# A fourth buffer for the halves of the projections' weights, and a ring of raw tiles that uses its first two tiles twice at its begin

## The chip, the cores and the metric

The kernel runs on one core of a Trainium2 chip. Its time is what the device takes for one execution, in microseconds (us). The median of three executions counts, and a change is looked at as the difference of two medians.

## The reference

A decoder layer over 1024 positions with a width of 1024. Three branches (an mLSTM, a differential attention, a cross-attention into 256 memory tokens) are each projected, weighted by a gate of their own and added, then an output projection and a residual follow, then an MLP with four times the width.

```python
g_m, g_d, g_c = jnp.split(jax.nn.sigmoid(h @ w_gate[l] + b_gate[l]), N_BRANCH, axis=-1)
merged = g_m * (y_m @ w_proj_m[l]) + g_d * (y_d @ w_proj_d[l]) + g_c * (y_c @ w_proj_c[l])
x = x + merged @ w_out[l]
h2 = rms_norm(x, norm_mlp_g[l])
x = x + jnp.square(jax.nn.relu(h2 @ w_up[l])) @ w_down[l]
```

The change touches what stands here: the three projections, the output projection, and the two products of the MLP. All of it is float32.

## The kernel before, in words

**Products in three.** Every float32 operand is split into a high part, a cast to fp32r on ScalarE, and a low part, the subtraction of that cast on VectorE (`split`, lines 111 and 112, and `split2`, lines 104 and 67, which keeps to the order of the program). A product is three matmuls: high with high, high with low, low with high (`mm3`, all at line 91). A weight or an operand is usable when both engines have passed it.

**The projections** (`tail`, from line 1410). There are sixteen groups: four for each of three branches, then four of the output projection. The weights of a group, 1024 x 256, come in two halves of four k each (`load_w`, line 130): SyncE loads a raw half (`raw`, two buffers, pool `rp2`), then it is split into a tile `w` (three buffers of 8 KB per partition, pool `wp2`, line 1445). I count the halves from 0 to 31, so a group uses halves 2g and 2g + 1, and half n takes the buffer n modulo 3. A group computes four tiles of 128 x 512, and each runs over all eight k: the first half of the weights is read until the middle of the fourth tile, the second to its end. Only the first group of each branch runs over k on the outside, since its eight tiles of y come in one by one (`k_tiles`, line 1376, `kraw` with two buffers, `kt`). In front of the sums of a branch a tile of gates is loaded (`gl`, two buffers), in the output projection one of x. There the residual sum is formed (`res`, line 1470, VectorE at line 1474), stored as x1, squared and added to `ssq` on GpSimd, and stored once more, weighted by the norm's gain, as h2. Sums have all eight banks of PSUM to go round.

**The up projection** (`wino`, line 1287) multiplies blocks of 2 x 2 with seven products in the place of eight. A step takes a raw weight tile of four blocks (`wraw`, SyncE, line 1272), forms four sums of them on GpSimd (`wino_s`, lines 1258 to 1261), splits seven (`wo`), and then runs 21 matmuls. I call the split weights W[0] to W[63] after their steps. An operand X[k], k from 0 to 3, is made of h2's rows of two tiles: a load (`xr`, one buffer), four differences (`wino_t`, lines 1240 to 1243), and two splits (`xo`). Run 0 has two steps (X[0], X[1]), run 1 four (X[0] to X[3]), run 2 two (X[2], X[3]), all further runs four. A run fills seven banks, and the eighth moves on by one from run to run. In run 0 the row sums of `ssq` go into the eighth bank (`px`), `st` (line 1531) copies them out, and the next run's first product uses that bank. After a run, VectorE combines its banks (`combine`, the tiles `u` and `c`), scales, and ScalarE applies the square of relu; the result is transformed like X and stored as an operand of the down projection (`r_d`).

**The down projection** (`down`, line 1558) does the same over 64 steps with three buffers for raw and split weights; its operands `xd` are read back from `r_d`. The first operand has three parts in three pools (`dx00`, `dx01`, `dx02`).

**Memory.** Pools lie one behind the other, and a pool of a later stage takes the place of those before. The raw tiles of w_up go round in four places, wr0 to wr3. wr0 and wr1 lie where the raw tiles of y (`kraw`) were, wr2 and wr3 lie in the last of the operands that the output projection reads to its end. The split weights lie in wop1 and three tiles of wop2; those three begin where the raw halves were and reach over the first two buffers of `wp2`. `xo0` and `xo1` (X[0] and X[1]) lie where the tiles of y were, `xo2` and `xo3` in operands of the output projection. In the down projection `dx02` takes the place of wr2 and wr3, and the first two raw tiles of w_down that of wr0 and wr1.

**Order.** A scheduler puts the instructions of the unpinned parts (the projections, and the begin of both products of the MLP) into an order for each engine, by when it thinks operands and buffers free; each engine then works its queue in that order. Within `wino` and `down` TensorE, VectorE and the casts are pinned to the order of the program.

Of the kernel before, what the change touches and what calls it, by code (L numbers as in the profile page):

```python
# [35 lines left out]
class Banks:  # L36


    def __init__(self, enter, name):
        self.pools = [enter(name=f"{name}{i}", bufs=1, space=PSUM) for i in range(8)]  # L40

    def tile(self, shape, dt, tag, name):
        return self.pools[int(tag[-1])].tile(shape, dt, tag=tag, name=name)


class Ring:


    def __init__(self, pools):
        self.pools, self.i = pools, -1  # L50

    def tile(self, *a, **k):
        self.i += 1
        return self.pools[self.i % len(self.pools)].tile(*a, **k)

# [16 lines left out]
class Layer:  # L72
# [487 lines left out]
    def m_gates2(self, pool):  # L560
# [5 lines left out]
        self.nc.vector.tensor_copy(self.gcol, ps2[:, 0 : 3 * W])  # L566

    def branch_m(self, pool, gp, tail, gnext):
        nc, a = self.nc, self.a
        V, G = nc.vector, nc.gpsimd  # L570
# [839 lines left out]
    def tail(self):  # L1410
# [11 lines left out]
        with ExitStack() as c0:  # L1422
            E = lambda *x, **k: c0.enter_context(tc.tile_pool(*x, **k))
# [8 lines left out]
            with ExitStack() as c1:  # L1432
                E = lambda *x, **k: c1.enter_context(tc.tile_pool(*x, **k))
                self.pmm, self.kmm, self.nmm = Banks(E, "pmm2"), 8, 3
                if True:
# [6 lines left out]
                    ysp = Ring([E(name=f"ys{i}", bufs=1) for i in range(9)][::-1])  # L1442
                    rawp = E(name="yrp", bufs=2)
                    self.rp = E(name="rp2", bufs=2)
                    self.wp = E(name="wp2", bufs=3)
                    hi = [[mtp.tile([P, 512], F32R, name=f"mh{k}_{hf}") for hf in range(2)] for k in range(NK)]
                    mg, lo = {}, {}
                    for bi, b in enumerate((2, 0, 1)):
# [41 lines left out]
            with ExitStack() as c1:  # L1490
                E = lambda *x, **k: c1.enter_context(tc.tile_pool(*x, **k))
# [4 lines left out]
                )  # L1496
                wop2 = [one_(f"wop2{i}") for i in range(3)]
                self.xop = (xo0, xo1, xo2, xo3)
                self.wrp, self.wop = Ring([wr0, wr1, wr2, wr3]), Ring([wop1, *wop2])
                dp, ap = one_("dgp"), one_("prt")  # L1500

                def load(kp):
# [395 lines left out]
```

## Time and profile before

| what | us |
|---|---|
| median of three executions | 2201.62 |
| lowest and highest of them | 2198.82, 2202.04 |
| the profiled execution | 2204.73 |
| its span, first to last instruction | 2203.0 |
| mean granted clock of TensorE in it | 0.995 of full |

The profile is that of one execution. PE is TensorE, PEld its weight loads, DVE VectorE, ACT ScalarE, POOL GpSimd, SP SyncE, and the q behind a name is an engine's own queue (issues of transfers). A row of the timeline has the start and the time from there to the end of the last instruction, the engine, the line, the operation, the tiles out<-in, the count, and in brackets the idle time before it with what ended it. Starts are us from the span's begin. The projections run from 1205.98, the output projection from about 1474, the up projection from 1565.70, the down projection from 1884.53.

### The profile page before, as it was taken

Reading aid. Unit: us, or ns where it says so; the run is one execution under the profiler, and the core shown is the slowest. Engines: PE = TensorE matmul, PEld = TensorE weight load, DVE = VectorE, ACT = ScalarE, POOL = GpSimd, SP = SyncE. Lnnn points to the kernel's source line nnn. Section 1 sums busy time; section 2 is a strip of 40 time slices with the busy share of each in tenths; the row PEclk is TensorE's granted clock in tenths of the full one; section 3 lists DMA queues with packets and bytes.
Section 4 is the critical chain, followed back from the end, with each engine's and each line's share of the span. In section 5 each row is a group of like instructions: output and inputs, shape, how many; then the busy total and the mean of one; then the engine's idle time right before and its main releaser. Section 6 shows DMA issues by size and latency. Waiting matters only on the chain.

```text
span 2203.0 us, 30700 instructions
## 1 busy us (share of the span) xinstructions
PE 2154.4 (98%) x11049; PEld 1853.4 (84%) x11049; DVE 1422.5 (65%) x2678; ACT 1002.2 (45%) x1998; POOL 561.1 (25%) x732
## 2 busy tenths in 40 slices
PE   7999999999999999999999999999999999999999
PEld 5878888898899999999887788887787888788887
DVE  6643565575547877877655332544689877767789
ACT  6543354454346666666554220323444444543332
POOL 2100000000111111111121002202657655565553
PEclk9999999999999999999999999999999999999999
DMA  7123122121443343333343543436435444854444
GB/s 250 31 78 110 59 92 68 47 79 48 169 107 92 96 96 97 87 78 88 115 149 130 181 154 114 143 106 210 149 111 199 158 147 147 323 196 153 144 142 169
DMA packets 137358, 281.46 MB, mean 128 GB/s; under 512 B 13137, under 2 KB 29814, under 8 KB 135158
## 3 DMA queue, kind: packets, MB, share of 16 engines
q1 hardware_dynamic: 130870, 259.58, 37.5%
q10 hardware_dynamic: 6336, 19.93, 2.2%
q8 instruction: 87, 1.43, 0.3%
q14 instruction: 65, 0.53, 0.1%
HBM read 182.95 MB, written 71.34 MB: 115 GB/s over the span
## 4 chain that ended last, share of the span: by engine, by line
PE 81%; DMA 6%; DVE 6%; ACT 3%; issue 2%; POOL 1%; SPq 0%; DVEq 0%; ACTq 0%; POOLq 0%
PE mm L91 47%; PE p L91 22%; PE sc L91 6%; PE po L91 3%; PE tp L94 3%; DMA kraw<-y 1%; DVE acc L67 1%; DVE w L112 1%; PE pr L94 1%; DVE wo L67 1%; DVE u L67 0%; PE tp L91 0%; DMA gl<-in_xT 0%; DMA x_d<-gl 0%; DVE xts L67 0%
## 5 line engine op out<-in xcount | busy, mean ns | idle before, releaser
L91 PE MATMUL mm<-w,hT 128*128 128x384 f32 (+3 forms) x2496 | 473.2, 332 | 3.5 <-ACT w L111 3.0
L91 PE MATMUL mm<-hT,w 128*128 128x512 f32 x1680 | 411.9, 396 | 0.0
L91 PEld LDWEIGHTS mm<-w,hT 128*128 128x128 f32 x2496 | 390.2, 190 | 15.4 <-ACT w L111 3.9
L91 PEld LDWEIGHTS mm<-hT,w 128*128 128x128 f32 x1680 | 308.5, 188 | 64.7
L91 PE MATMUL p<-xo,wo 128*128 128x512 f32 x1344 | 309.8, 392 | 6.4 <-DVE st L1531 3.5
L91 PE MATMUL p<-xd,wo 128*128 128x512 f32 x1344 | 309.0, 392 | 4.8 <-DVE u L67 2.0
L91 PEld LDWEIGHTS p<-xo,wo 128*128 128x128 f32 x1344 | 252.2, 189 | 62.6 <-ACT pt L1344 3.9
L91 PEld LDWEIGHTS p<-xd,wo 128*128 128x128 f32 x1344 | 253.4, 189 | 60.2 <-DVE u L67 2.8
L91 PE MATMUL mm<-kt,w 128*128 128x512 f32 x1152 | 264.5, 391 | 5.1 <-ACT kt L111 3.5
L91 PEld LDWEIGHTS mm<-kt,w 128*128 128x128 f32 x1152 | 216.8, 189 | 52.7 <-ACT kt L111 4.3
L111 ACT CAST w<-raw 128x256 fp32r<-128x256 f32 (+3 forms) x272 | 142.1, 545 | 163.3 <-PE mm L91 122.5
L112 DVE TENSOR_TENSOR w<-raw,w 128x256 fp32r<-128x256 f32 (+3 forms) x272 | 161.8, 616 | 75.6 <-ACT w L111 74.9
L104 ACT CAST wo<-wraw 128x896 fp32r<-128x896 f32 x122 | 115.0, 944 | 209.5 <-PE p L91 110.2
L67 DVE TENSOR_TENSOR wo<-wraw,wo 128x896 fp32r<-128x896 f32 x122 | 143.6, 1194 | 59.3 <-ACT wo L104 59.3
L1258 POOL TENSOR_TENSOR wraw<-wraw 128x128 f32<-128x128 f32 x128 | 94.2, 736 | 246.6 <-DMA wraw<-in_wdown 119.8
L1006 ACT ACTIVATE dpe<-sc,dst,drr 128x256 f32<-128x256 f32 (+7 forms) x128 | 106.6, 833 | 97.6 <-DVE dst L1002 95.3
L127 POOL TENSOR_SCALAR hss<-hss 128x4 f32<-128x4 f32 x8 | 3.3, 407 | 416.8 <-ACT mscr L752 273.1
L998 DVE CUSTOM_DVE_ANT_0 sc<-sc,tmask 128x256 f32<-128x256 f32 (+7 forms) x128 | 97.0, 758 | 13.1 <-PE sc L91 12.4
L91 PE MATMUL sc<-dk,dq 128*128 128x512 f32 (+3 forms) x384 | 92.2, 348 | 0.0
L1261 POOL TENSOR_TENSOR wraw<-wraw 128x128 f32<-128x128 f32 x128 | 87.0, 680 | 10.0
L1260 POOL TENSOR_TENSOR wraw<-wraw 128x128 f32<-128x128 f32 x128 | 88.6, 692 | 0.0
L104 ACT CAST xd<-xd 128x1536 fp32r<-128x1536 f32 (+2 forms) x36 | 54.9, 1528 | 69.9 <-DMA xd<-r_d 69.9
(308 smaller groups left out, 3086.0 us busy)
## 6 DMA issues: line engine op xcount, KB each, us to landing
dk<-dsg SPq DMA_DIRECT2D x64, 256.0 KB, 4.5
wraw<-in_wup SPq DMA_DIRECT2D x64, 256.0 KB, 3.2
r_d<-xts SPq DMA_DIRECT2D x16, 1024.0 KB, 4.1
wraw<-in_wdown SPq DMA_DIRECT2D x64, 256.0 KB, 3.0
xd<-r_d SPq DMA_DIRECT2D x19, 768.0 KB, 7.2
xd<-r_d SPq DMA_DIRECT2D x14, 1024.0 KB, 6.7
raw<-in_wd SPq DMA_DIRECT2D x32, 384.0 KB, 3.2
kraw<-y SPq DMA_DIRECT2D x24, 512.0 KB, 4.2
```

The source lines that it names most:

```text
L67: return self.tc.keep_in_program_order(f(*a, **k))
L91: self.pin(self.nc.tensor.matmul(out, l, r, start=start, stop=stop))
L94: self.pin(self.nc.tensor.transpose(out, x, self.ident))
L104: self.A.copy(hi, src)
L111: nc.scalar.copy(hi, src)
L112: nc.vector.tensor_sub(lo, src, f32(hi))
L127: g.tensor_scalar(r, ss, 1.0 / width, EPS, op0=ALU.mult, op1=ALU.add)
L998: V.tensor_tensor_reduce(out=sc[:, 0:n], in0=sc[:, 0:n], in1=self.tmask[:, D - n : D], scale=1.0, scalar=-3.0e38, op0=ALU.add, op1=ALU.max ...
L1006: nc.scalar.activation(pe[c][:, 0:n], sc[:, 0:n], AF.Exp, bias=t8[:, 2 + c : 3 + c], scale=rr[:, i, c : c + 1], accum_out=t8[:, 4 + c : 5 ...
L1258: G.tensor_add(r[:, 4], r[:, 0], r[:, 3])
L1260: G.tensor_sub(r[:, 6], r[:, 1], r[:, 0])
L1261: G.tensor_sub(r[:, 7], r[:, 2], r[:, 5])
```

## The change

The pool `wp2` gets four buffers, so half n takes the buffer n modulo 4. And the ring of the raw tiles of w_up starts again after its first two tiles, once: wr0, wr1, wr0, wr1, wr2, wr3, wr0 and so on, where it went wr0, wr1, wr2, wr3, wr0. The other rings keep their order. All of `wp2`'s fourth buffer lies behind the last pool of the stage, so no other pool moves.

```diff
     def __init__(self, pools, again=0):
-        self.pools, self.i = pools, -1
+        self.pools, self.i, self.again = pools, -1, again

     def tile(self, *a, **k):
+        if self.i == self.again - 1:
+            self.i, self.again = -1, 0
         self.i += 1
         return self.pools[self.i % len(self.pools)].tile(*a, **k)
...
-                    self.wp = E(name="wp2", bufs=3)
+                    self.wp = E(name="wp2", bufs=4)
...
-                self.wrp, self.wop = Ring([wr0, wr1, wr2, wr3]), Ring([wop1, *wop2])
+                self.wrp, self.wop = Ring([wr0, wr1, wr2, wr3], 2), Ring([wop1, *wop2])
```

The change itself is in buffers alone; what it moves is seen in the order. Line numbers are higher by two in the changed kernel. First VectorE between the first and the second group of the output projection, before; w_15103 and w_15108 are the third group's halves, gl_ are residual sums, xts and xo belong to X[0].

```order
L112 TENSOR_TENSOR w_14958<-raw_14956,w_14958 128x1024
L1474 SCALAR_TENSOR_TENSOR gl_14915<-mm_14815,gl_14915 128x512
L1474 SCALAR_TENSOR_TENSOR gl_14923<-mm_14816,gl_14923 128x512
L112 TENSOR_TENSOR w_15103<-raw_15101,w_15103 128x1024
L1474 SCALAR_TENSOR_TENSOR gl_14931<-mm_14817,gl_14931 128x512
```

And further on in the same queue, before, behind X[0]:

```order
L112 TENSOR_TENSOR xo_15522<-xts_15517,xo_15522 128x4x512
L1474 SCALAR_TENSOR_TENSOR gl_15091<-mm_15066,gl_15091 128x512
L112 TENSOR_TENSOR w_15108<-raw_15106,w_15108 128x1024
L112 TENSOR_TENSOR w_15253<-raw_15251,w_15253 128x1024
L1474 SCALAR_TENSOR_TENSOR gl_15136<-mm_15111,gl_15136 128x512
```

The same two places after the change:

```order
L114 TENSOR_TENSOR w_15103<-raw_15101,w_15103 128x1024
L1476 SCALAR_TENSOR_TENSOR gl_14915<-mm_14815,gl_14915 128x512
L1476 SCALAR_TENSOR_TENSOR gl_14923<-mm_14816,gl_14923 128x512
L114 TENSOR_TENSOR w_15108<-raw_15106,w_15108 128x1024
L1476 SCALAR_TENSOR_TENSOR gl_14931<-mm_14817,gl_14931 128x512
```

```order
L114 TENSOR_TENSOR xo_15522<-xts_15517,xo_15522 128x4x512
L1476 SCALAR_TENSOR_TENSOR gl_15091<-mm_15066,gl_15091 128x512
L114 TENSOR_TENSOR w_15253<-raw_15251,w_15253 128x1024
L114 TENSOR_TENSOR w_15258<-raw_15256,w_15258 128x1024
L114 TENSOR_TENSOR wo_15527<-wraw_15509,wo_15527 128x7x128
```

Each half has moved up by about one place of its kind: w_15108 stands where w_15103 stood, and the last half (w_15258) and the split of W[1] (wo_15527), which followed further on, stand behind X[0].

Next SyncE at the end of the output projection, before; wraw_15530 and wraw_15560 are the raw tiles of W[2] and W[3], xr_15675 the load for X[3].

```order
L1484 DMA h_d<-h_2487_15363 128x512
L1272 DMA wraw_15530<-in_wup 128x512
L1272 DMA wraw_15560<-in_wup 128x512
L1475 DMA x_d<-gl_15391 128x512
L1484 DMA h_d<-h_2491_15398 128x512
L1504 DMA xr_15675<-h_d 128x2x1024
```

After, with wraw_15569 and wraw_15606 as the raw tiles of W[4] and W[5]:

```order
L1486 DMA h_d<-h_2487_15363 128x512
L1274 DMA wraw_15569<-in_wup 128x512
L1274 DMA wraw_15606<-in_wup 128x512
L1477 DMA x_d<-gl_15391 128x512
L1486 DMA h_d<-h_2491_15398 128x512
L1506 DMA xr_15675<-h_d 128x2x1024
```

The two pairs have changed places: those of W[2] and W[3] now stand where those of W[4] (right behind that of W[1]) and W[5] stood. On VectorE and ScalarE the splits of W[2] and W[3] keep their places, behind X[2] and ahead of `st`.

Last VectorE in the combination after the last run but one of the up projection, and at the last run's, before; xd_18250 is the third part of the down projection's first operand, xd_18273 and xd_18275 are its second operand, xd_18290 a part of the third; wo_18270, wo_18277 and wo_18294 are its first three split weights; p are banks.

```order
L67 TENSOR_TENSOR u_2827_17989<-u_2825_17987,p_2814_17866 128x512
L67 TENSOR_TENSOR c_2828_17990<-u_2827_17989,p_2815_17867 128x512
L67 TENSOR_TENSOR u_2827_17989<-u_2827_17989,p_2816_17868 128x512
L67 TENSOR_TENSOR u_2825_17987<-u_2825_17987,p_2816_17868 128x512
L67 TENSOR_TENSOR u_2825_17987<-u_2825_17987,p_2817_17869 128x512
```

```order
L112 TENSOR_TENSOR wo_18270<-wraw_18252,wo_18270 128x7x128
L112 TENSOR_TENSOR xd_18250<-xd_18250 128x2x512
L112 TENSOR_TENSOR xd_18273<-xd_18273 128x3x512
L112 TENSOR_TENSOR xd_18275<-xd_18275 128x4x512
L67 TENSOR_TENSOR c_2841_18117<-u_2840_18116,p_2832_18017 128x512
L112 TENSOR_TENSOR wo_18277<-wraw_18258,wo_18277 128x7x128
L67 TENSOR_TENSOR u_2840_18116<-u_2840_18116,p_2833_18018 128x512
L112 TENSOR_TENSOR wo_18294<-wraw_18280,wo_18294 128x7x128
L67 TENSOR_TENSOR u_2842_18118<-u_2840_18116,p_2834_18019 128x512
L112 TENSOR_TENSOR xd_18290<-xd_18290 128x3x512
L67 TENSOR_TENSOR c_2843_18119<-u_2842_18118,p_2835_18020 128x512
```

After:

```order
L69 TENSOR_TENSOR u_2827_17989<-u_2825_17987,p_2814_17866 128x512
L114 TENSOR_TENSOR xd_18250<-xd_18250 128x2x512
L69 TENSOR_TENSOR c_2828_17990<-u_2827_17989,p_2815_17867 128x512
L69 TENSOR_TENSOR u_2827_17989<-u_2827_17989,p_2816_17868 128x512
L69 TENSOR_TENSOR u_2825_17987<-u_2825_17987,p_2816_17868 128x512
```

```order
L114 TENSOR_TENSOR wo_18270<-wraw_18252,wo_18270 128x7x128
L114 TENSOR_TENSOR xd_18273<-xd_18273 128x3x512
L114 TENSOR_TENSOR xd_18275<-xd_18275 128x4x512
L69 TENSOR_TENSOR c_2841_18117<-u_2840_18116,p_2832_18017 128x512
L114 TENSOR_TENSOR wo_18277<-wraw_18258,wo_18277 128x7x128
L69 TENSOR_TENSOR u_2840_18116<-u_2840_18116,p_2833_18018 128x512
L69 TENSOR_TENSOR u_2842_18118<-u_2840_18116,p_2834_18019 128x512
L114 TENSOR_TENSOR wo_18294<-wraw_18280,wo_18294 128x7x128
L69 TENSOR_TENSOR c_2843_18119<-u_2842_18118,p_2835_18020 128x512
L114 TENSOR_TENSOR xd_18290<-xd_18290 128x3x512
```

The split of xd_18250 has moved into the combination of the last run but one, and in that of the last run the sums stand further ahead of the splits. On SyncE the load of xd_18250 has moved ahead of the first raw tile of w_down, and the second raw tile behind the second operand. At the begin of the projections, not shown, ScalarE casts the fifth half ahead of the fifth tile of y, and TensorE has more matmuls of the second group ahead of that tile.

More of the change, by code (lines that the diff above doesn't have):

```diff
@@ L46, with __init__ @@
 class Ring:
-    def __init__(self, pools):
-        self.pools, self.i = pools, -1
+    def __init__(self, pools, again=0):
+        self.pools, self.i, self.again = pools, -1, again
     def tile(self, *a, **k):
+        if self.i == self.again - 1:
+            self.i, self.again = -1, 0
         self.i += 1
```

## The prediction

> **What bounds the kernel now.** I read the page's busy shares first, then the waits of TensorE, then its granted clock in windows of 10 us, and last the timelines of all engines around each wait.
>
> ```profile
> PE 2154.4 (98%) x11049; PEld 1853.4 (84%) x11049; DVE 1422.5 (65%) x2678; ACT 1002.2 (45%) x1998; POOL 561.1 (25%) x732
> ```
>
> TensorE is busy 98% of the span, so an edit that leaves its matmuls alone can win only its idle time, and the time in which its clock is low. The waits name the places (us in all, times, longest):
>
> ```profile
> PE mm L91 <- DVE w L112: 3.7, 3, 2.7
> PE p L91 <- DVE u L67: 3.6, 4, 2.0
> PE p L91 <- DVE st L1531: 3.5, 1, 3.5
> PE mm L91 <- ACT kt L111: 3.5, 2, 2.3
> ```
>
> The first and the last lie in the projections, the third at the begin of the up projection, the longest of the second at its end: all near tiles that the change touches. The windows give busy us, the granted clock (third number), and the DMA share:
>
> ```profile
> 1210.00:1220.00 10.00, 7.70 (x28) 0.83 0.82 296
> 1520.00:1530.00 10.00, 7.26 (x32) 1.00 0.70 228
> 1580.00:1590.00 10.00, 9.29 (x34) 0.83 0.18 58
> 1890.00:1900.00 10.00, 7.83 (x21) 0.66 0.67 239
> ```
>
> Waiting costs twice at three of these places: 10 x (1 - 0.83) = 1.7 us of full-speed work is lost to the clock at 1210 and at 1580, and 3.4 us at 1890. The window at 1520 lost none, though a wait lies in it.
>
> **Output projection.** Timeline of TensorE, then of VectorE:
>
> ```profile
> 1524.25 0.74 PE L91 MATMUL mm<-mh,w 128*128 128x512 f32 x2 [2.74 <-DVE w L112]
> 1546.97 0.73 PE L91 MATMUL mm<-mh,w 128*128 128x512 f32 x2 [0.63 <-DVE w L112]
> ```
> ```profile
> 1498.65 1.22 DVE L112 TENSOR_TENSOR w<-raw,w 128x1024 fp32r<-128x1024 f32 x1 [2.71 <-ACT w L111]
> 1522.50 3.92 DVE L112 TENSOR_TENSOR w<-raw,w 128x1024 fp32r<-128x1024 f32 x2
> ```
>
> The 2.74 us are a wait for the second half of the third group (w_15108), split at 1522.5. With three buffers it reuses that of the second group's first half, so its split comes late and stands behind the split of X[0]. With four it reuses that of the first group's second half, and stands on ScalarE and VectorE in the slot that w_15103 has now, 1498.65, some 20 us before its use. The last half (w_15258) follows in the slot of 1522.5, where TensorE needs it only at 1546.97 - 0.63 - 2.74 = 1543.6. Both waits go: 2.74 + 0.63 = 3.4 us. The splits themselves are as many as before, and VectorE's idle time hides them. Without that cover each would cost its 1.2 us. In SyncE's queue the loads of the halves pass single loads of gates and of x; those feed sums for which eight banks are there, and TensorE waits for none of them now.
>
> **Begin of the up projection.** TensorE, SyncE, GpSimd, then VectorE:
>
> ```profile
> 1565.70 6.28 PE L91 MATMUL p<-xo,wo 128*128 128x512 f32 x27
> ...
> 1580.71 16.06 PE L91 MATMUL p<-xo,wo 128*128 128x512 f32 x63 [3.49 <-DVE st L1531]
> ```
> ```profile
> 1566.53 1.03 SPq L1272 DMA_DIRECT2D wraw<-in_wup  x2
> ```
> ```profile
> 1577.21 1.18 POOL L1261 TENSOR_TENSOR wraw<-wraw 128x128 f32<-128x128 f32 x1
> ```
> ```profile
> 1536.76 0.69 DVE L1240 TENSOR_TENSOR xts<-xr 128x512 f32<-128x512 f32 x1 [3.68 <-DMA xr<-h_d]
> ...
> 1560.17 0.69 DVE L1240 TENSOR_TENSOR xts<-xr 128x512 f32<-128x512 f32 x1 [8.19 <-DMA xr<-h_d]
> ...
> 1568.53 0.69 DVE L1474 SCALAR_TENSOR_TENSOR gl<-mm,gl 128x512 f32<-128x512 f32 x1 [4.16 <-DMA gl<-in_xT]
> ...
> 1572.45 2.56 DVE L112 TENSOR_TENSOR xo<-xts,xo 128x2048 fp32r<-128x2048 f32 x1 [1.57 <-POOL wraw L1258]
> 1576.89 1.20 DVE L112 TENSOR_TENSOR wo<-wraw,wo 128x896 fp32r<-128x896 f32 x1 [1.88 <-ACT wo L111]
> 1579.40 1.09 DVE L67 TENSOR_TENSOR wo<-wraw,wo 128x896 fp32r<-128x896 f32 x1 [1.31 <-ACT wo L104]
> 1580.41 0.16 DVE L1531 COPY st<-px 128x8 f32<-128x8 f32 x1
> ```
>
> Run 1 may start when the copy st has emptied its bank, and st stands on VectorE behind the splits of W[2] and W[3]. Their raw tiles lie in wr2 and wr3, memory that the output projection reads to its end. So they are loaded at 1566.53, summed on GpSimd until 1578.4, split, and only then st follows. In the changed program both lie in wr0 and wr1 and are loaded long before: the first in the slot of SyncE's queue that W[4]'s tile has now, behind the same split of W[0], so that nothing behind it waits longer. VectorE then has, after the last subtraction of X[2] (1572.45 + 2.56 = 1575.0), two splits of 1.1 us and st: without any shift 1577.4 at the latest.
>
> What comes late next is X[2] itself. It hangs on h2's stores, on its load (the wait that ended at 1560.17) and on the last residual sum (1568.53). Seen in the times of the trace, TensorE arrives 3.4 us earlier: 1577.2 - 3.4 = 1573.8. If X[2] moves as far, st ends at 1574.0 and nothing is waited for. If it does not move, run 1 starts at 1577.5. I take 2.7 us for X[2]: w_15258's 1.2 us leave VectorE's queue between X[1] and the residual sum that X[2]'s load waits for, and in SyncE's queue no load of weights, held by its buffer, stands before X[1]'s last store of h2 any more, as one does now, for which I estimate 1.5 us out of the 3.68 us that X[1] waited. Then run 1 starts at 1574.7, not 1580.7: 6.0 us over both waits, with bounds 3.2 and 6.7. The 0.9 us that remain are a third of the 2.74 us that left the clock at 1.00. So I add the 1.7 us of clock, with 0 as the lower bound. W[4] and W[5] take over the loads at 1566.53 and are needed two steps later than W[2] was, 2 x 21 matmuls at (6.28 - 0.39) / 26 = 0.227 us, which is 9.5 us. (0.39 is a matmul's own duration.) This place gives 7.7 us.
>
> The Trainium skill, TensorE: Matmul & The Clock Gate, section "HAM oscillation", says that gaps under about 3.4 us keep the clock. The row at 1210 speaks against it as a guarantee: the longest wait there is 2.30 us, and the clock fell. By that rule the 1.7 us would come even at a remaining wait of 3 us; by the row they might not.
>
> **First group of the projections.** TensorE, ScalarE, and the landing times of the y loads (512 KB each):
>
> ```profile
> 1215.06 16.64 PE L91 MATMUL mm<-kt,w 128*128 128x512 f32 x64 [2.30 <-ACT kt L111]
> 1232.86 29.41 PE L91 MATMUL mm<-kt,w 128*128 128x512 f32 x128 [1.17 <-ACT kt L111]
> ```
> ```profile
> 1222.91 1.05 ACT L111 CAST w<-raw 128x1024 fp32r<-128x1024 f32 x1 [2.13 <-PE mm L91]
> ```
> ```profile
> DMA to landing us min/median/max: 3.2/4.2/6.2
> ```
>
> The first wait stays, for the third tile of y is loaded as before. The fourth buffer lets TensorE take 10 matmuls of the second group ahead of the fifth tile. But the cast that waits until 1222.91 for a buffer now stands ahead of the fifth tile's on ScalarE, which leaves it at about 1225. Ten matmuls, 2.3 us from 1222.9, cover just that. The seventh tile's load waits for the fifth's split, 1225.0 + 1.2 = 1226.2, and lands 3.2 to 6.2 us later. With its cast it is there at 1230.5 to 1233.5, 1231.5 at the median; TensorE gets there after 27 more matmuls, 1225.1 + 27 x 0.227 = 1231.2. That wait of 0.3 us (0 to 2.3) comes off the 1.17 us won. I take +0.9, bounds -1.1 and +1.2. Everywhere else in the projections TensorE doesn't wait, and the buffer wins nothing.
>
> **From up to down.** With the ring's two extra uses, the last four raw tiles lie in wr2, wr3, wr0, wr1 instead of wr0 to wr3. The third part of the down projection's first operand (xd_18250, in the place of wr2 and wr3) loads earlier, and the first two raw tiles of w_down load later. TensorE, then VectorE:
>
> ```profile
> 1884.53 1.52 PE L91 MATMUL p<-xd,wo 128*128 128x512 f32 x6
> ...
> 1891.47 1.65 PE L91 MATMUL p<-xd,wo 128*128 128x512 f32 x3 [1.95 <-DVE u L67]
> 1893.81 6.36 PE L91 MATMUL p<-xd,wo 128*128 128x512 f32 x18 [0.69 <-DVE c L67]
> ```
> ```profile
> 1857.99 2.61 DVE L67 TENSOR_TENSOR wo<-wraw,wo 128x896 fp32r<-128x896 f32 x2
> ...
> 1864.80 0.69 DVE L67 TENSOR_TENSOR c<-u,p 128x512 f32<-128x512 f32 x1
> ...
> 1880.48 1.23 DVE L112 TENSOR_TENSOR xd<-xd 128x1024 fp32r<-128x1024 f32 x1 [2.66 <-ACT xd L111]
> ...
> 1886.12 0.68 DVE L67 TENSOR_TENSOR c<-u,p 128x512 f32<-128x512 f32 x1
> ...
> 1889.73 1.09 DVE L112 TENSOR_TENSOR wo<-wraw,wo 128x896 fp32r<-128x896 f32 x1 [1.25 <-ACT wo L111]
> ...
> 1891.34 1.83 DVE L112 TENSOR_TENSOR xd<-xd 128x1536 fp32r<-128x1536 f32 x1
> ```
>
> The landing time of xd_18250 among the issues of 1856 to 1896, the channels' share ahead of that, and the landing times of all the loads of operands here:
>
> ```profile
> xd<-r_d SPq DMA_DIRECT2D x1, 512.0 KB, 7.2
> ```
> ```profile
> 1863.00:1871.00 8.00, 8.00 (x37) 1.00 0.03 10
> ```
> ```profile
> DMA to landing us min/median/max: 4.5/9.1/13.8
> ```
>
> xd_18250 can start at 1857.99 + 2.61 = 1860.6. It took 7.2 us among full queues; where it goes now, the DMA share is 0.03, so I take the 4.2 us of a y tile. Cast and subtraction, about 2.3 us, now stand before the sum of 1864.80, which so ends near 1867.8. TensorE needs that bank 15 matmuls into the last run, 84 x 0.227 us before 1884.53 plus 3.4, at 1868.9. So it is just hidden, at 7.2 us it costs 2. At the end, 1.23 us less stand before the sum of 1886.12, and two of the four sums that TensorE waits for no longer stand behind the third split of w_down (1889.73). But the other two still do, the last of them behind the subtraction of 1891.34 too. I expect the matmuls after them, now 1893.81 to 1895.1, some 1 us earlier, with most of the 3.4 us of clock lost again. I take +1.0, with bounds -4 (a 2 us wait, its clock, and later loads behind) and +4 (the clock kept).
>
> **Sum.** 7.7 + 0.9 + 1.0 = 9.6 us. The profiled execution took 2204.73 us, span 2203.0, so 2195.1; against the median of 2201.62 I forecast 2192.0.
>
> **Rivals.**
> - X[2] takes the place: loads and stores at the end of the output projection hold it where it is. For it: the residual sum at 1568.53 waited 4.16 us for a load. Run 1 then starts at 1577.5, 3.2 us early, the wait is as long as now, and the clock falls. 3.2 + 0.9 + 1.0 = 5.1 us: 2196.5. Chance 0.16.
> - xd_18250 lands after 7 us or more, and VectorE's and ScalarE's queues hold the sums of the last but one run behind it. About -4 instead of +1.0: 4.6 us won, 2197. Chance 0.10.
> - The same at its worst, the slower side: a landing of 13.8 us, the longest at this place, ends the sum at 1877.4, 8.5 us after TensorE wants it. With 1.7 to 3.4 us of clock and the raw tiles of w_down later by as much, about 13 us against 8.6 won: 2206. It decides from a landing of some 11 us on. Against it: the share of 0.03. Chance 0.04.
> - The change does not reach the waits, since the splits keep their late places behind X[0]: the time stays at 2201.6. The order speaks against it. Chance 0.04.
> - Both boundaries run clean and keep the clock: 3.4 + 3.5 + 1.7 + 1.2 + 4 = 13.8 us, 2187.8. Chance 0.06.
>
> My forecast has the remaining 0.60. The range 2187.5 to 2198.0 takes in its bounds and the first two rivals. A measurement of this kernel tells about 0.2%, 4.4 us, from no change. Faster by that: 0.60, 0.06, most of the first rival, half of the second, 0.79. Within: 0.18. Slower: 0.03.
>
> **What the changed profile would show.** No wait for w at L112 in the output projection; run 1 starting after less than 1.5 us of wait, with a clock of 1.00 in the 10 us behind it; W[2]'s and W[3]'s sums on GpSimd before 1540; xd_18250's cast some 5 us behind its issue, with no wait in the last run of the up projection. A wait there of 2 us or more, or a wait for xo at run 1, would make me wrong.

## The result and the profile after

| what | before | after |
|---|---|---|
| median, us (22 executions each) | 2203.9 | 2197.95 |
| lowest to highest | 2198.82 to 2208.01 | 2192.48 to 2205.47 |
| ratio to before, 95% interval | | 0.9971 (0.9963 to 0.9979) |
| the profiled execution, us | 2204.73 | 2198.07 |
| its span, us | 2203.0 | 2196.3 |

(The median of 2201.62 us given ahead of the prediction is that of the first three of the 22.) The change makes the kernel about 6 us faster (0.29%; the interval gives 4.6 to 8.2 us); the forecast was 9.6 us. The median of 2197.95 us lies at the upper end of the stated range of 2187.5 to 2198.0. The lines of the changed kernel's code lie two further on. TensorE's waits (us in all, times, longest):

```profile
PE p L93 <- DVE u L69: 3.5, 4, 1.9
PE mm L93 <- ACT kt L113: 2.7, 2, 2.1
PE px L93 <- POOL ssq L1483: 1.7, 1, 1.7
PE px L93 <- ACT rb L1544: 0.6, 1, 0.6
PE px L93 <- DVE gl L1476: 0.5, 1, 0.5
```

The waits for `w` in the output projection and for `st` are gone. Three waits of `px` are new; `px` are the short matmuls that sum the squares over the partitions (`px<-ones,ssq`) and later spread the result (`px<-dg,ones`). The windows of 10 us (busy, granted clock, DMA share, GB/s):

```profile
1210.00:1220.00 10.00, 7.75 (x28) 0.87 0.97 349
1570.00:1580.00 10.00, 9.37 (x38) 0.83 0.65 220
1890.00:1900.00 10.00, 10.00 (x39) 0.84 0.76 265
```

The clock still falls at all three places. At the begin of the up projection it falls in the window ahead of the one where it did, and at the end it falls by half as much (0.66 before).

To compare executions I cut the tail into four stretches at rows that every kernel has: the first matmul on y (`kt`), the first `p` matmul, the `p` matmul behind the second group of `px<-dg,ones`, the first `p` matmul on `xd`, and the span's end. TensorE's timeline before, two of these rows (1565.70 and 1884.53 stand in the prediction):

```profile
1205.98 1.17 PE L91 MATMUL mm<-kt,w 128*128 128x512 f32 x4 [0.72 <-POOL ones L1426]
...
1601.05 14.31 PE L91 MATMUL p<-xo,wo 128*128 128x512 f32 x62
```

TensorE's timeline after:

```profile
1206.78 1.17 PE L93 MATMUL mm<-kt,w 128*128 128x512 f32 x4 [1.00 <-POOL ones L1428]
...
1215.80 16.42 PE L93 MATMUL mm<-kt,w 128*128 128x512 f32 x63 [2.15 <-ACT kt L113]
...
1561.12 6.28 PE L93 MATMUL p<-xo,wo 128*128 128x512 f32 x27
1567.93 1.02 PE L93 MATMUL px<-ones,ssq 128*128 128x1 f32 x8 [0.53 <-DVE gl L1476]
1570.63 1.05 PE L93 MATMUL px<-ones,ssq 128*128 128x1 f32 x8 [1.67 <-POOL ssq L1483]
...
1596.44 18.88 PE L93 MATMUL p<-xo,wo 128*128 128x512 f32 x82
...
1880.07 2.20 PE L93 MATMUL p<-xd,wo 128*128 128x512 f32 x9
```

- Projections (from `kt` to the first `p`): 1565.70 - 1205.98 = 359.7 us before, 1561.12 - 1206.78 = 354.3 after. 5.4 us are won.
- Begin of up (to the `p` behind the second group of `px<-dg,ones`): 1601.05 - 1565.70 = 35.4, and 1596.44 - 1561.12 = 35.3. Nothing is won.
- Steady up: 283.5 and 283.6. In every kernel below it lies between 283.2 and 284.1, so the table leaves it out.
- End: 2203.0 - 1884.53 = 318.5, and 2196.3 - 1880.07 = 316.2. 2.2 us are won.

So the whole question is the begin of up, where the forecast had 4.3 us (6.0 for both waits and 1.7 of clock, less the 3.4 that lie in the output projection). VectorE's timeline there, after:

```profile
1567.09 0.69 DVE L1476 SCALAR_TENSOR_TENSOR gl<-mm,gl 128x512 f32<-128x512 f32 x1 [4.03 <-DMA gl<-in_xT]
...
1571.01 2.54 DVE L114 TENSOR_TENSOR xo<-xts,xo 128x2048 fp32r<-128x2048 f32 x1 [1.56 <-POOL wraw L1260]
1573.47 1.34 DVE L114 TENSOR_TENSOR wo<-wraw,wo 128x896 fp32r<-128x896 f32 x1
1574.74 1.34 DVE L69 TENSOR_TENSOR wo<-wraw,wo 128x896 fp32r<-128x896 f32 x1
1576.01 0.15 DVE L1533 COPY st<-px 128x8 f32<-128x8 f32 x1
```

W[2] and W[3] are split right behind X[2], as the change meant it. But TensorE came 4.6 us earlier (1561.12 for 1565.70), and the last residual sum only 1.44 us (1567.09 for 1568.53), as did X[2]'s last subtraction (1571.01 for 1572.45). (These are times from the span's begin. The tail began 0.8 us later in this execution; counted from its first matmul on y, TensorE came 5.4 us earlier and the sum and X[2] 2.2.) That sum still waited 4.03 us for its tile of x. X[2]'s two subtractions stand right behind it in VectorE's queue, the splits of W[2] and W[3] and `st` behind those; and through the last sum of squares on GpSimd it holds up `px`.

### The profile page after: what moved, and what is told of

Same layout as the page of the kernel before. It is cut to its first block, busy times and chain, and to the rows that moved or that the text cites. A ratio compares the mean times of both kernels' runs of the same rounds, so it can differ in the third digit from the quotient of the medians.

```text
span 2196.3 us, 30710 instructions
## 1 busy us (share of the span) xinstructions
PE 2154.0 (98%) x11049; PEld 1853.4 (84%) x11049; DVE 1424.0 (65%) x2678; ACT 1002.6 (46%) x1998; POOL 571.6 (26%) x732
## 4 chain that ended last, share of the span: by engine, by line
PE 79%; DMA 7%; DVE 6%; ACT 3%; POOL 2%; issue 2%; SPq 0%; DVEq 0%; ACTq 0%; POOLq 0%
PE mm L93 46%; PE p L93 21%; PE sc L93 6%; PE po L93 3%; PE tp L96 3%; DMA x_d<-gl 1%; DVE acc L69 1%; DVE wo L69 1%; DMA gl<-in_xT 1%; PE pr L96 1%; DMA xr<-h_d 1%; DVE u L69 1%; DMA kraw<-y 1%; POOL wraw L1262 0%; DVE w L114 0%
## 5 line engine op out<-in xcount | busy, mean ns | idle before, releaser
L93 PE MATMUL p<-xd,wo 128*128 128x512 f32 x1344 | 307.8, 391 | 3.8 <-DVE u L69 1.9
L1260 POOL TENSOR_TENSOR wraw<-wraw 128x128 f32<-128x128 f32 x128 | 95.1, 743 | 238.4 <-DMA wraw<-in_wdown 103.5
L1263 POOL TENSOR_TENSOR wraw<-wraw 128x128 f32<-128x128 f32 x128 | 93.9, 733 | 10.0
L1262 POOL TENSOR_TENSOR wraw<-wraw 128x128 f32<-128x128 f32 x128 | 91.8, 717 | 0.0
```

Of the source, the lines that this page charges most:

```text
L93: self.pin(self.nc.tensor.matmul(out, l, r, start=start, stop=stop))
L1260: G.tensor_add(r[:, 4], r[:, 0], r[:, 3])
L1262: G.tensor_sub(r[:, 6], r[:, 1], r[:, 0])
L1263: G.tensor_sub(r[:, 7], r[:, 2], r[:, 5])
```

## The experiments

My theory: the chain of the last residual sum and X[2] bounds the begin of up once W[2] and W[3] are early, and it is held by the load of x, for which there are two buffers (`gl`). So the two parts of the change meet there. The rivals: the parts just add, the wait of `px` is a price by itself, or X[2] is bound by something else. All ratios are to the kernel before, on the same chip (1 to 4 on one chip, 5 to 8 on a second, 9 to 12 on a third). The same code ahead of the tail differed by several us between the profiled executions (the last matmul ahead of the first `kt` matmul ended at 1202.6 to 1210.2). A ratio's interval is some 2 to 3 us to either side, so I read the place from the stretches, which come from one execution of each kernel. The first stretch begins with the first matmul on y, so it leaves out the wait ahead of that matmul: 0.3 to 1.0 us in the kernels before, changed and 1 to 7, but 3.34 us in kernel 8, 2.52 in 9 to 11 and 1.41 in 12.

| kernel | ratio (interval) | projections | begin of up | end |
|---|---|---|---|---|
| before | 1 | 359.7 | 35.4 | 318.5 |
| changed | 0.9971 (0.9963 to 0.9979) | 354.3 | 35.3 | 316.2 |
| 1 buffer alone | 0.9990 (0.9981 to 0.9999) | 355.0 | 36.9 | 318.9 |
| 2 ring alone | 0.9980 (0.9969 to 0.9991) | 361.6 | 31.1 | 316.6 |
| 3 changed, px later | 0.9971 (0.9959 to 0.9982) | 355.2 | 34.2 | 317.0 |
| 4 changed, third gl | 0.9939 (0.9927 to 0.9951) | 351.6 | 31.1 | 316.8 |
| 5 changed, third x | 0.9961 (0.9946 to 0.9976) | 352.4 | 32.3 | 319.9 |
| 6 changed, hole larger | 0.9962 (0.9949 to 0.9976) | 351.4 | 37.7 | 318.5 |
| 7 as 5, no ring | 0.9960 (0.9947 to 0.9974) | 352.8 | 33.7 | 319.1 |
| 8 as 4, third y | 0.9933 (0.9920 to 0.9945) | 349.9 | 31.3 | 316.5 |
| 9 as 8, no ring | 0.9963 (0.9950 to 0.9976) | 348.3 | 32.2 | 319.5 |
| 10 as 8, three w | 0.9977 (0.9964 to 0.9990) | 356.8 | 30.4 | 316.2 |
| 11 as 8, neither | 0.9992 (0.9982 to 1.0001) | 355.9 | 32.2 | 319.5 |
| 12 as 5, hole larger | 0.9946 (0.9934 to 0.9959) | 351.4 | 32.4 | 316.0 |

**1. The buffer alone.**

```diff
-self.wrp, self.wop = Ring([wr0, wr1, wr2, wr3], 2), Ring([wop1, *wop2])
+self.wrp, self.wop = Ring([wr0, wr1, wr2, wr3]), Ring([wop1, *wop2])
```

> Only the fourth buffer for halves of the projections' weights; the ring of raw tiles as before. My theory: the begin of the up projection takes back most of what the buffer wins, since W[2] and W[3] still lie in memory that the output projection reads to its end and st stands behind their splits. TensorE reaches the first p matmul about 5 us earlier than before (1561 instead of 1565.7), the wait for st is again 2 to 6 us, the clock falls as before in the 10 us behind it, and the end of up is as before (waits 0.7 and 1.9, clock about 0.66 behind them). Ratio to the kernel before 0.9985 to 0.9995 (1 to 3 us faster). Rival, the two parts just add: all 5.4 us that the changed kernel won up to the first p matmul stay, ratio 0.9975.

TensorE's timeline at the begin of up:

```profile
1570.97 1.25 PE L93 MATMUL px<-ones,ssq 128*128 128x1 f32 x8 [1.67 <-POOL ssq L1483]
...
1579.57 14.56 PE L93 MATMUL p<-xo,wo 128*128 128x512 f32 x63 [2.39 <-DVE st L1533]
```

As the theory has it: 4.7 us are won in the projections (359.7 to 355.0), 1.5 are given back at once (35.4 to 36.9), 0.5 at the end, and by the ratio (0.9990) 2.2 us remain. The rival's 0.9975 lies outside the interval. Both bounds, the `px` behind X[2]'s sum and the `st` behind W[3], stand here one behind the other.

**2. The ring alone.**

```diff
-self.wp = E(name="wp2", bufs=4)
+self.wp = E(name="wp2", bufs=3)
```

> Only the ring's two extra uses of its first tiles; three buffers for halves as before. My theory: the waits of the first group (2.3 and 1.2) and of the output projection (2.7 and 0.6) are as before, but at run 1 TensorE, which arrives late, waits for st at most 0.5 us and keeps its clock (1.00 in 1580 to 1590), and the end of up gains 1.6 to 2. So 3.0 to 3.5 for the wait, 1.7 for the clock, 1.6 for the end: about 6 us faster, ratio 0.9970 to 0.9977, as much as both parts together, because the parts overlap. Rival, the parts add: the ring brings only what is left of the change beyond the 5.4 us up to the first p matmul, some 1 us, ratio 0.9993 to 1.0.

TensorE's timeline in the output projection and at the begin of up:

```profile
1522.66 0.50 PE L93 MATMUL mm<-mh,w 128*128 128x512 f32 x1 [0.71 <-ACT w L113]
1526.39 0.73 PE L93 MATMUL mm<-mh,w 128*128 128x512 f32 x2 [3.00 <-DVE w L114]
...
1576.31 17.99 PE L93 MATMUL p<-xo,wo 128*128 128x512 f32 x78
```

And the window behind those waits (busy, granted clock, DMA share, GB/s):

```profile
1520.00:1530.00 10.00, 6.29 (x22) 0.87 0.54 166
```

Run 1 of the up projection begins within the unbroken stretch from 1576.31: no wait for `st`, 4.2 us won at the begin of up (35.4 to 31.1), and 1.9 at the end. In its output projection the wait was 3.00 us right behind one of 0.71, and the clock in 1520 to 1530 was 0.87 and not 1.00, which is part of the 1.8 us that the projections took longer. The ratio, 4.4 us with 2 to 7 in the interval, is a little below what I expected. It doesn't say that the parts overlap: 2.2 + 4.4 = 6.6 us is what both bring together. The overlap is seen only in the stretch at the begin of up: 4.2 us by the ring alone, 1.6 (36.9 to 35.3) with the buffer. Over the whole tail, from the first matmul on y to the end, it isn't seen: the parts bring 2.4 and 4.0 us, both together 7.5. So the rival that the parts just add is not ruled out for the total time of the change.

**3. The sums of squares later.**

```diff
-if (r, kp, j) in ((0, 1, 1), (1, 1, 6), (1, 2, 6), (1, 3, 3)):
+if (r, kp, j) in ((0, 1, 5), (1, 1, 6), (1, 2, 6), (1, 3, 3)):
```

> The changed kernel with the eight px matmuls on the sums of squares four steps later in run 0 (after the 17th group of three p matmuls of X[1], not the 13th). My theory: X[2], W[2] and W[3] bound the begin of up. The px waits (0.53 and 1.67) vanish and come back as a wait for st, W[2] or X[2] ahead of run 1; the time is that of the changed kernel within 1 us (ratio to before 0.9968 to 0.9978), with the low clock behind the new wait. Rival, the wait of px for ssq on GpSimd is itself the price: 2.2 us and the 1.7 us of clock are won, 2 to 4 us faster than the changed kernel, ratio 0.9953 to 0.9962.

TensorE's timeline:

```profile
1570.47 1.84 PE L93 MATMUL px<-ones,ssq 128*128 128x1 f32 x16
...
1575.68 15.87 PE L93 MATMUL p<-xo,wo 128*128 128x512 f32 x63 [2.56 <-DVE st L1533]
```

The waits of `px` have become one of 2.56 us for `st`, which stands behind X[2], W[2] and W[3]. The ratio is that of the changed kernel, though its interval reaches the rival's upper end (0.9962). So `px` only shows a bound that lies elsewhere.

**4. A third buffer for tiles of gates and x.** The down projection's pad is larger by the same 2 KB, so that its tiles keep their places.

```diff
-self.gl = E(name="gl", bufs=2)
+self.gl = E(name="gl", bufs=3)
...
-accum(a0, 2, 128)
+accum(a0, 2, 640)
```

> The changed kernel with a third buffer for gates and x tiles (gl), and the pad in the down projection's memory larger by as much. The loads of gates and x stand one place earlier in SyncE's queue against the weights' halves. My theory: the last residual sum (now 1567.09, 4.03 us waiting for its load) no longer waits for the load, h2's last store and with it X[2]'s load, subtraction, W[2], W[3] and st come about 2.5 us earlier, and so do ssq and px: the px waits (0.53 and 1.67) go, and the clock behind them stays near 1. About 2 to 4 us faster than the changed kernel, ratio to before 0.9952 to 0.9962. Rival, px waits for ssq, whose GpSimd sums have their own length, and X[2] for its earlier load: no change against the changed kernel, ratio 0.9968 to 0.9978.

The last load of x in SyncE's queue, then TensorE's first `p` matmul, then the last residual sum and `st` on VectorE:

```profile
1554.18 0.33 SPq L1420 DMA_DIRECT2D gl<-in_xT  x1
```
```profile
1559.08 6.28 PE L93 MATMUL p<-xo,wo 128*128 128x512 f32 x27
```
```profile
1559.33 0.69 DVE L1476 SCALAR_TENSOR_TENSOR gl<-mm,gl 128x512 f32<-128x512 f32 x1 [1.42 <-ACT sq L1482]
...
1568.94 0.15 DVE L1533 COPY st<-px 128x8 f32<-128x8 f32 x1
```

The load is issued 5 us ahead of the sum, the sum waits for no load and comes 0.25 us behind the first `p` matmul, where it came 5.97 us behind it (1567.09 - 1561.12). `st` comes 7 us earlier (1568.94 for 1576.01), no `px<-ones,ssq` waits, and the begin of up takes 31.1 us. That is more than I expected, since the first group became better too: the pools behind `gl` moved by 2 KB, and the y tiles are loaded ahead of the weights (351.6 for 354.3). The next two kernels part these.

**5. The third buffer for x alone**, in memory behind the projections' weights.

```diff
-def fetch(d, f, hf):
-    t = self.gl.tile([P, 512], F32, tag="gl", name=self.name("gl"))
+def fetch(d, f, hf, pool=None):
+    t = (pool or self.gl).tile([P, 512], F32, tag="gl", name=self.name("gl"))
...
+gx = Ring([self.gl, self.gl, E(name="gx", bufs=1)])
...
-x = fetch(a["xT"], f, hf)
+x = fetch(a["xT"], f, hf, gx)
```

> The changed kernel with a third buffer for the x tiles of the residual sums alone, in memory behind the projections' weights, so that no other tile moves and TensorE's order is the same. It parts the two things that the kernel with a third gl did: its first group also became better (waits 0.51 + 0.46 + 1.45 at full clock, in place of 0.18 + 2.15 + 0.51 with the clock at 0.87). My theory: the first group is as in the changed kernel, the last residual sum waits for no load any more, X[2]'s last subtraction and st come 4 to 7 us earlier, and from the first p matmul to the end of the second group of px on dg pass 31.1 instead of 35.3 us. 4.2 us faster than the changed kernel, ratio to before 0.9952 (0.9946 to 0.9960). Rival: the gain came from the first group, and X[2] is bound by the loads' landing: no more than 1 us, 0.9967 to 0.9975.

TensorE's timeline, a wait that is new at the begin of up, and those at the end; and the windows behind the first three of these and behind the last:

```profile
1591.35 2.56 PE L93 MATMUL p<-xo,wo 128*128 128x512 f32 x10 [0.99 <-DVE wo L69]
...
1882.66 1.71 PE L93 MATMUL p<-xd,wo 128*128 128x512 f32 x6 [1.36 <-POOL wraw L1263]
1885.03 0.96 PE L93 MATMUL p<-xd,wo 128*128 128x512 f32 x3 [0.66 <-DVE c L69]
1887.90 17.05 PE L93 MATMUL p<-xd,wo 128*128 128x512 f32 x72 [1.90 <-DVE u L69]
1906.56 18.69 PE L93 MATMUL p<-xd,wo 128*128 128x512 f32 x74 [1.61 <-DVE acc L69]
```
```profile
1890.00:1900.00 10.00, 10.00 (x46) 1.00 0.81 289
1900.00:1910.00 10.00, 8.24 (x29) 0.85 0.98 340
```

No `px<-ones,ssq` waits, and the begin of up falls from 35.3 to 32.3; a wait of 0.99 for a split weight has come in. At the end the clock held in 1890 to 1900 (1.00, 0.84 in the changed kernel), but TensorE then waited 1.61 us for an accumulator, and behind that wait the clock fell after all (0.85 in 1900 to 1910). The end took 3.7 us more than in the changed kernel; how much of that belongs to the edit was not tried. The ratio alone can't tell this kernel from the changed one.

**6. The first group alone.**

```diff
-hole = E(name="hole", bufs=1).tile([P, 7 * 256], F32, name="hole")
+hole = E(name="hole", bufs=1).tile([P, 9 * 256], F32, name="hole")
```

> The changed kernel with 2 KB more in the hole ahead of the projections' y tiles and weights, and nothing else: the loads of the first group's y tiles come ahead of those of its weights, as in the kernel with a third gl, and two buffers serve the x tiles as in the changed kernel. My theory: TensorE reaches the first p matmul some 2.5 us earlier than in the changed kernel, and most of it is given back at the begin of up, where X[2] bounds (longer px waits for gl and ssq, or a wait for st or xo): 0 to 1.5 us faster than the changed kernel, ratio to before 0.9964 to 0.9972. Rival: X[2]'s chain moves with TensorE and the gain stays: 0.9957 to 0.9962.

TensorE's timeline:

```profile
1566.77 1.02 PE L93 MATMUL px<-ones,ssq 128*128 128x1 f32 x8 [2.68 <-DVE gl L1476]
1569.47 1.87 PE L93 MATMUL px<-ones,ssq 128*128 128x1 f32 x8 [1.68 <-POOL ssq L1483]
```

TensorE gains 3.0 us in the projections (354.3 to 351.4), and 2.3 of them are gone at the begin of up (35.3 to 37.7): `px` waits 4.36 us for the same chain where it waited 2.20. This is the theory's clearest row, since nothing at that place was changed. The ratio, from 1 us slower to 5 us faster than the changed kernel, holds both expectations.

**12. Both of these together.** The edits of 5 and 6.

> The changed kernel with the third x buffer and with the 2 KB more in the hole (the better order in the first group), which measured 0.9961 and 0.9962 each by itself against 0.9971 for the changed kernel. My theory: each alone is held by the other's place (TensorE early finds X[2] late; X[2] early is of use only as far as TensorE is early), so together they bring more than the sum of the two, as the third gl did: ratio to the kernel before 0.9936 to 0.9946, with no px wait and 31.1 us from the first p matmul to the end of the second group of px on dg. Rival, they add: 0.9948 to 0.9956.

0.9946, at the end of the first expectation and within reach of the rival's 0.9948 to 0.9956. The stretches say that each place kept its gain (351.4 and 32.4), the ratio can't say whether they do more than add. Its interval doesn't meet that of the changed kernel, nor does that of kernel 4: third x buffer and better first group together are worth some 5 to 7 us.

**7. The third x buffer without the ring.** The edits of 1 and 5.

> The fourth buffer and the third x buffer, without the ring's extra uses. My theory: the third x buffer alone doesn't open the begin of up, since W[2] and W[3] lie in memory that the output projection reads to its end, and st stands behind their splits. X[2] is early, the px waits go, and a wait for st of 3 to 6 us is left, with the clock down to about 0.83 behind it; from the first p matmul to the end of the second group of px on dg pass 35 to 37 us, as with the buffer alone (36.9). Ratio to before 0.9983 to 0.9993. Rival, the ring matters at this place only through X[2]: 31 to 32 us there, ratio 0.9960 to 0.9968 (only the end of up is worse).

TensorE's timeline, GpSimd's (the last of the sums for W[3]), and the window:

```profile
1575.12 14.56 PE L93 MATMUL p<-xo,wo 128*128 128x512 f32 x63 [3.31 <-DVE st L1534]
```
```profile
1571.62 1.18 POOL L1263 TENSOR_TENSOR wraw<-wraw 128x128 f32<-128x128 f32 x1
```
```profile
1570.00:1580.00 10.00, 6.70 (x29) 1.00 0.51 179
```

The wait for `st` came back as expected, 3.31 us, behind W[3], whose sums ended at 1572.8. But the clock did not fall, and the ring's own two waits (0.99 for `wo` and 0.62 for `rb` in kernel 5) were absent. So the ring was worth 1.4 us there (33.7 to 32.3), not 3 to 5, and the ratios of 5 and 7 are alike. My expectation of the time was wrong by 5 us or more: it had counted the clock in, and another 2 us lie in the projections (352.8 for 355.0 in kernel 1), where nothing of this edit acts. The rival's ratio (0.9960 to 0.9968) is what was measured, but not for its reason alone: the place took 33.7 us and not its 31 to 32.

**8. A third buffer for raw y tiles** on top of kernel 4, which measures the first group.

```diff
-rawp = E(name="yrp", bufs=2)
+rawp = E(name="yrp", bufs=3)
```

> The kernel with a third gl (ratio 0.9939) and a third buffer for raw y tiles too: the eight y loads of the first batch come ahead of more of the weights. My theory, the first group waits for y loads that wait for a raw buffer: its waits (0.46 + 1.45) go, 1 to 2 us faster than with a third gl, ratio to before 0.9930 to 0.9935. Rival, the DMA engines are full there (share 0.95 to 0.97 in 1200 to 1220), so the loads only change places and the halves of the weights come later: no gain, or a wait for w of 1 to 3 us, ratio 0.9939 to 0.9955.

TensorE's timeline:

```profile
1207.12 33.20 PE L93 MATMUL mm<-kt,w 128*128 128x512 f32 x138 [3.34 <-issue]
```

From its first matmul on y TensorE waits for nothing for 33 us. But it waited 3.34 us ahead of that matmul, where kernel 4 waited 0.84. Counted with this wait the projections take 353.3 us, in kernel 4 352.5, so the 1.7 us that the stretch shows (351.6 to 349.9) are no gain by the profile. The cast of the first half of the weights ended at 1207.0, right ahead of that first matmul, which is what the rival said: the loads change places and the weights come later. By the ratio this is the fastest kernel of the study, 0.9933, but the difference from kernel 4 is within the intervals.

**9 to 11. The change on the ground of kernel 8.** Here neither y nor X[2] binds, and TensorE's order is the same in all four kernels. Taken out are the ring's extra uses (9), the fourth buffer (10), or both (11), by the edits of 1 and 2.

> The kernel with third gl and y buffers (ratio 0.9933, all its runs within 2.6 us), with the ring's two extra uses taken out; TensorE's order is the same. My theory: X[2] stays early, so what comes back at the begin of up is the wait for st behind the late W[2] and W[3], 3 to 4 us (3.3 in the kernel with a third x buffer and no ring), with up to 1.7 us of clock, and at the end of up 2 us: 5 to 7 us slower than with the ring, ratio to the kernel before 0.9955 to 0.9965. Rival, with X[2] early the ring no longer matters (the kernels with a third x buffer measured 0.9961 with the ring and 0.9960 without): 0.9930 to 0.9940.

> The kernel with third gl and y buffers, with three buffers for the projections' halves again in place of four; TensorE's order is the same. My theory: the waits in the output projection come back, 2.7 to 3.0 and 0.6 to 0.7 us, and up to 1.3 us of clock; at the begin of up TensorE comes late and nothing waits. 3.4 to 5 us slower than with four, ratio to the kernel before 0.9949 to 0.9956. Rival, the buffer won its time only where y and x loads were late: 0.9930 to 0.9938.

> The kernel with third gl and y buffers without either part of the change, so that the change can be measured on a ground where neither y nor X[2] binds. My theory: what the parts bring adds up here, because nothing behind them takes it back: 5 to 7 for the ring and 3.4 to 5 for the buffer, 8.4 to 12 us slower than with both, ratio to the kernel before 0.9971 to 0.9988. Rival, the parts overlap as in the changed kernel's begin of up: 5 to 7 us slower, 0.9955 to 0.9966.

TensorE's timeline without the ring (9), and without the buffer (10):

```profile
1566.72 8.44 PE L93 MATMUL p<-xo,wo 128*128 128x512 f32 x36 [1.79 <-DVE st L1533]
```
```profile
1518.53 0.73 PE L93 MATMUL mm<-mh,w 128*128 128x512 f32 x2 [2.52 <-DVE w L114]
1541.92 0.50 PE L93 MATMUL mm<-mh,w 128*128 128x512 f32 x1 [1.79 <-ACT w L113]
1544.39 0.73 PE L93 MATMUL mm<-mh,w 128*128 128x512 f32 x2 [1.73 <-DVE w L114]
```

Without the ring: 0.9963, as expected, though the wait for `st` was 1.79 us and not 3 to 4, with no loss of clock. The stretches show 0.9 us more at the begin of up and 3.0 at the end, and 1.6 less in the projections; some 4 of the ratio's 6.6 us are in no row of the profiled execution, which was the fastest of its six. So the expected time came out, and its mechanism is shown only in part. Without the buffer: 0.9977, about 10 us slower than kernel 8, twice what I expected. Its profile shows 6.9 us in the projections and 1.2 less behind them; the rest of the 10 is in no stretch. The last half now costs 1.79 + 1.73 us where it cost 0.63 before, and the clock fell behind them. Without both: 0.9992. The rival, that the parts overlap, had 0.9955 to 0.9966 and falls: by the ratios the parts cost 6.6 and 9.7 us, both together 13, so within the intervals they add here.

On this ground the change takes the kernel from 0.9992 to 0.9933, 0.59% or 13 us; on its own ground it took 0.29%. The profiled executions show less of a difference: from the first matmul on y to the end the change takes off 9.2 us here (990.7 to 981.5) and 7.5 on its own ground (997.0 to 989.5). That it is worth twice as much rests on the ratios alone. And for the buffers for gates, x and y, without the change, the ratio shows nothing that is clear of noise (0.9992, up to 1.0001).

## Why the prediction was right and wrong

**Output projection: right. First group: not shown.** Forecast 3.4 + 0.9 = 4.3 us, measured 5.4. The waits for `w` are gone, also a third one of 0.31 us that the forecast left out. Those for `kt` went from 2.30 + 1.17 to 2.15 + 0.51. But kernels 1 and 3 have the same four buffers, and there they were 2.48 + 0.99 and 2.87 + 0.80, no less than before. So the 0.9 us of the first group may be luck of one execution. Kernel 1 shows 4.7 us with the buffer alone, of which 3.7 are waits that went.

**Begin of up: wrong.** The failing step is the one from "TensorE arrives 3.4 us earlier" and "I take 2.7 us for X[2]" to "The 0.9 us that remain". It lets TensorE gain 0.7 us on X[2]; TensorE gained 3.1. X[2]'s last subtraction moved 1.44 us, or 2.2 counted from the tail's first matmul, which is not far from the 2.7. TensorE moved 4.6 us, or 5.4 counted so: the step left out the 0.9 us that the forecast itself gave to the first group, and these are lost again at a place that X[2] holds. I had named the last residual sum's wait of 4.16 us in the first rival and yet moved X[2] by the shifts ahead of it in VectorE's and SyncE's queues, as if it could follow TensorE. The load of that sum is not held by these: it needs one of two `gl` buffers, which the store of the tile two before has to free. SyncE's queue after, then what its loads of `gl` waited for between 1540 and 1572 (us in all, times, longest):

```profile
1561.73 0.32 SPq L1477 DMA_DIRECT2D x_d<-gl  x1
1563.07 0.32 SPq L1486 DMA_DIRECT2D h_d<-h  x1
1563.70 0.33 SPq L1420 DMA_DIRECT2D gl<-in_xT  x1
```
```profile
SPq L1420 <- DMA x_d<-gl: 10.3, 5, 6.9
```

That store comes late, because its residual sum stands on VectorE behind the differences of X[2], which wait for their own load; the tile's load follows 2 us behind the store and lands at 1567, and X[2]'s subtractions stand in VectorE's queue behind the sum that it feeds. (In the expectation of kernel 4 I put X[2]'s load behind that sum. It is the subtractions that stand there.) Kernels 4 and 5 show that this is what holds X[2]: with a third buffer the sum waits for no load and the place gives 4.2 us in kernel 4, where the forecast wanted 4.3, and 3.0 in kernel 5.

**A wait that the prediction did not list.** `px<-ones,ssq` passed in the kernel before right behind the end of its last sum of squares (1572.05), so no row showed it as a wait; with TensorE 4.6 us earlier it waited 2.20 us. Kernel 3 shows that it is no price of its own: moved away, its wait turns up at `st`.

**Clock at the begin of up: wrong.** The forecast counted 1.7 us as won, because a remaining wait of 0.9 us would be short. The waits were 0.53 and 1.67 us and the window stood at 0.83.

**End of up: right in sign and place, too small in size.** Forecast +1.0, measured 2.2. Of these 1.0 us is idle time of TensorE that went (9.5 to 8.4 us in the stretch), as forecast, and 1.2 are shorter matmul time (309.0 to 307.8), since the clock fell less, where the forecast had it fall as before. SyncE's queue and ScalarE after:

```profile
1856.17 0.38 SPq L1612 DMA_DIRECT2D xd<-r_d  x1
```
```profile
1859.85 1.05 ACT L113 CAST xd<-xd 128x1024 fp32r<-128x1024 f32 x1 [1.91 <-DMA xd<-r_d]
```

xd_18250 was issued when I took it to be (1856.17, which with the 4.5 us that were won by then is 1860.7, against 1860.6), was there 3.7 us later (4.2 assumed), and TensorE has no wait in the last run of up. The longest wait behind it is as before (1.9 us); why the clock fell less was not tried. The ring has this gain in seven of the nine kernels that have it (316.0 to 317.0, without it 318.5 to 319.5); in the other two (5 and 6) TensorE waits 1.6 and 1.5 us for an accumulator there.

**Sum.** 4.3 + 4.3 + 1.0 was forecast, 5.4 + 0.0 + 2.2 came out of the stretches, less 0.8 us by which the tail began later in the profiled execution. The first rival's mechanism came true at its place. Its 5.1 us lie within the measured 4.6 to 8.2 us, where the forecast's 9.6 do not; the other two terms were larger than it had them.

## What to carry to other kernels

An engine that arrives earlier by several us makes new bounds of the steps that just fitted: list for each the row that ends closest ahead of it, not only those that show a wait. When a step is to move, follow its load back to the buffer that it needs and to who frees that buffer; a queue's order says nothing of that. A change can be worth more once the next bound is opened (0.59% for 0.29% by the ratios here), so measure the two together before either is dropped.

## What the runs showed of the hardware

The length of a single wait doesn't tell whether the clock falls. TensorE's window of 10 us in kernel 3, around its one wait of 2.56 us:

```profile
1570.00:1580.00 10.00, 7.44 (x35) 0.83 0.54 190
```

There 2.56 us cost 1.7 us of clock, while 3.31 us in kernel 7 and 2.74 us in the kernel before cost nothing, and in the kernel before 3.49 us did. Nor do several waits close to each other tell: 0.53 and 1.67 us within 3 us cost it in the changed kernel, and 1.79 and 1.73 us in kernel 10, whose window is this:

```profile
1540.00:1550.00 10.00, 6.47 (x21) 0.83 0.44 153
```

But 1.36, 0.66 and 1.90 us within 6 us left it at 1.00 in kernel 5, and the one wait of 1.61 us that came 17 us later there took it to 0.85 over 10 us, as one of 1.52 us did in kernel 6 (0.83). The Trainium skill, TensorE: Matmul & The Clock Gate, section "HAM oscillation", has gaps over about 3.4 us as those that bite; here one of 2.56 us and one of 1.61 us did, and one of 3.31 us, close to that figure, did not. What decides was not settled. A forecast should carry the 1.7 us as a bound for any wait of about 1.5 us or more, and count it neither as lost nor as won.
